# Column products for the gating input and the queries: two activation parts side by side, wide and narrow matmuls, sums on VectorE, attention calls at other slots

## The chip, the cores and the metric

The kernel runs on one core of one Trainium2 chip. The core has a matrix engine (TensorE, "PE" in the profile; its weight loads are listed apart as "PEld"), a vector engine (VectorE, "DVE"), a scalar engine (ScalarE, "ACT"), a general engine (GpSimd, "POOL") and a queue that starts transfers (SyncE, "SP"). Each works through its own instructions in order, and they wait for each other with semaphores. Matmuls write to PSUM, which has eight banks of 512 float32 per partition; everything else works in SBUF. The metric is the time of one execution on the device in microseconds (us).

## The reference

The model is a decoder trunk of two layers on 256 positions with 1024 features, in float32. A layer is an FFN, a mixing sub-layer and a second FFN, each between two RMS norms:

```
h = rms_norm(x, ffn1_pre_g);  x = x + 0.5 * rms_norm(swiglu(h, w1, w2), ffn1_post_g)
h = rms_norm(x, mix_pre_g)
q, k, v, u_s, v_s, g_a, g_b = split(h @ w_in)
y_attn = sliding_window_attention(q, k, v, sinks)        # 16 query heads, 2 key/value heads, window 128
y_sgu  = spatial_gating(gelu(u_s), gelu(v_s), ...)       # u * (tril(W) layer_norm(v) + b), chunks of 128
merged = sigmoid(g_a) * (y_attn @ w_attn_branch) + sigmoid(g_b) * (y_sgu @ w_sgu_branch)
x = x + rms_norm(merged @ w_out, mix_post_g)
h = rms_norm(x, ffn2_pre_g);  x = x + 0.5 * rms_norm(swiglu(h, ...), ffn2_post_g)
```

The change is about two of the products with `w_in`: `u_s`, the gating input, and `q`, the queries, each 1024 features wide.

## The kernel before

**Products.** A float32 product is made of three products of TensorE's rounded format (float32r). Each operand is split into a high part, its rounded copy, and a low part, the rest: x = xh + xl and w = wh + wl. The product is xh·wh + xl·wh + xh·wl. The activations of a sub-layer lie transposed in one tile `xt` of 8 blocks of 128 features, and in each block the 256 positions of the high part are followed by the 256 of the low part. Three helpers form products. `row_major` (L266, through `passes`, L254) keeps activations as the stationary operand and streams weights, and its result has positions as rows. `feature_major` (L256) and `feature_pair` (L276) keep a block of weights stationary and stream activations, and the result has features as rows. `feature_major` takes three matmuls of 256 columns for each of 8 blocks, 24 in all, and sums everything in one half of a bank (lines L261, L262 and L263). `feature_pair` streams both parts of a block at once as 512 columns against wh, and the high part as 256 columns against wl: 8 wide and 8 narrow matmuls (L284). The bank then holds two halves, which must still be added. Before the change only the middle of the FFNs (`FFN.middle`, L637) uses it: there ACT copies the second half of the bank out (L650) and DVE adds the first half to the copy (L651).

**Weights.** The stream `st` (L102 on) brings the weights in units of 128 x 1024. SP starts a transfer into one of four raw buffers, ACT makes the high part `wh` (L140), DVE the low part `wl` (L154). Nine units fit the ring, and a unit is split up to AHEAD + 1 = 8 units ahead of its product; the low part of a unit is issued when the next unit is split (`low`, L148). After its product a unit's place becomes free (`done`).

**The mixing sub-layer** (`Mix.middle`, L806) works off 48 units in numbered slots: 0 to 7 the gating input u, 8 to 15 the queries q, 16 to 23 the gate g_b, 24 to 31 the gating branch, 32 to 39 the gate g_a, 40 to 47 the attention branch. `beside` (L818) issues for a slot first what is due at its start, then the product, then what is due at its second half, and then splits the next unit. What is due is held in a table by half-slots, and `go` (L813) runs a generator until its next `yield n`, which puts the rest n half-slots later. So the order of the instructions on every engine is fixed by hand; nothing is decided at run time.

`pairs` (L831) makes two units in the two halves of one bank and then starts the evacuation at the second half of the slot after them. For u this is one Gelu on ACT into `ut` (L873). For q it is `evac_q` (L883): ACT scales the two halves of the partitions by 0.125 into the high parts (L887), and one half-slot later DVE forms the low parts (L890), so that each head gets high and low part one above the other.

In slots 9 to 12 `gating` (L700) puts 8 matmuls of 128 columns on PE (L706) ahead of the slot's product, then two DVE steps (L710, L713), an ACT copy (L715) and a DVE step (L717). The keys' two transposes (L393) come at slot 3.

`attend` (L720) is called six times per layer, for each key/value head once for the first 128 positions (eight heads in one call) and twice for the second 128 (four heads each). ATTEND (L59) holds the half-slots at which the calls start. A call issues scores on PE (L736, L737); 3 half-slots later maxima on DVE (L743); 1 later exponentials on ACT (L756); 3 later the sums on DVE and the division on POOL (L764); 4 later transposes on PE (L773), split by ACT and DVE; 5 later the products with the values on PE (L785, L786); and then four short steps on ACT and DVE. The first call of a layer needs the queries of units 0 to 3 of q.

**Buffers.** The pool `mm` (L85) has 8 banks; the pool `t2` (L79) has 6 buffers of 512 float32 per partition, which the gating, attention and FFN steps share.

Of the kernel before, what the change touches and what calls it, by code (L numbers as in the profile page):

```python
# [16 lines left out]
AF = mybir.ActivationFunctionType  # L17
ALU = mybir.AluOpType
PSUM = bass.MemoryType.PSUM

P = 128
D = 1024
KD = D // P
S = 256
# [31 lines left out]

WARM = (11, 8)

ATTEND = (27, 32, 38, 44, 50, 56)  # L59
GATING = (9, 10, 11, 12)  # L60

GATE = (31, 33)
# [3 lines left out]
def trunk(ctx: ExitStack, tc: tile.TileContext, a: dict, out: bass.AP):  # L66
    nc = tc.nc

    def pool(name, bufs, **kw):
        return ctx.enter_context(tc.tile_pool(name=name, bufs=bufs, **kw))  # L70
# [8 lines left out]
    t2 = pool("t2", 6)  # L79
# [11 lines left out]
    def new(p, shape, tag, dt=F32, **kw):  # L91
        ids[0] += 1
        return p.tile(shape, dt, tag=tag, name=f"{tag}_{ids[0]}", **kw)

    def f(ap):
        return ap.bitcast(F32)

    def flat(ap):
        return ap.rearrange("p a b -> p (a b)")
# [67 lines left out]
    st = Stream()  # L167
# [45 lines left out]
    def bank():  # L213
        return new(mm, [P, 512], "mm")
# [38 lines left out]
        for i in which:  # L253
            nc.tensor.matmul(o, every[i][0], every[i][1], start=start and i == 0, stop=stop and i == 2)  # L254

    def feature_major(o, u, ah, al):  # L256

        wh, wl = st[u]
        for k in range(KD):
            ks = slice(k * P, (k + 1) * P)  # L260
            nc.tensor.matmul(o, wh[:, ks], ah[:, k, :], start=(k == 0), stop=False)  # L261
            nc.tensor.matmul(o, wh[:, ks], al[:, k, :], start=False, stop=False)  # L262
            nc.tensor.matmul(o, wl[:, ks], ah[:, k, :], start=False, stop=(k == KD - 1))  # L263
        st.done(u)

    def row_major(o, u, m, ah, al):  # L266

        wh, wl = st[u]
        for t in range(NT):
            for i in range(2):  # L270
                k, ws = 2 * m + i, slice(i * 512, (i + 1) * 512)
                passes(o[t], ah[:, k, rows_of(t)], al[:, k, rows_of(t)], wh[:, ws], wl[:, ws], (0, 1, 2),
                       k == 0, k == KD - 1)
        st.done(u)

    def feature_pair(o, u, both):  # L276

        wh, wl = st[u]

        wide = [(o, wh, flat(both[:, k]), k) for k in range(KD)]  # L280
        narrow = [(o[:, 0:S], wl, both[:, k, 0, :], k) for k in range(KD)]
        todo = wide[:-1] + narrow + wide[-1:]
        for i, (out_, w, x, k) in enumerate(todo):
            nc.tensor.matmul(out_, w[:, k * P:(k + 1) * P], x, start=(i == 0), stop=(i == len(todo) - 1))  # L284
        st.done(u)
# [334 lines left out]
    class FFN:  # L620
# [16 lines left out]
        def middle(self, xt, xth, xtl, turn1, early):  # L637
            for _ in range(2):
                self.into.append((new(m8, [P, 8, S], "m8", F32R), new(m8, [P, 8, S], "m8", F32R)))
            for c in range(FA, FC):  # L640
                o = [bank(), bank()]
                us = self.cols[(c - FA) * 2:(c - FA) * 2 + 2]
                for half in range(2):
                    feature_pair(o[half], us[half], xt)
                if c == FA + 2:
                    turn1()
                s = new(t2, [P, 512], "t2")
                y = s.rearrange("p (a b) -> p a b", a=2)
                for half in range(2):
                    nc.scalar.copy(y[:, half, :], o[half][:, S:2 * S])  # L650
                    nc.vector.tensor_tensor(out=y[:, half, :], in0=o[half][:, 0:S], in1=y[:, half, :], op=ALU.add)  # L651
                    if half == 0:
                        nc.scalar.activation(y[:, 0, :], y[:, 0, :], AF.Silu)  # L653
                nc.vector.tensor_tensor(out=y[:, 1, :], in0=y[:, 0, :], in1=y[:, 1, :], op=ALU.mult)
                st.upto(us[1] + 1 + AHEAD)
                hh, hl = self.lhs(c)
                split(hh, hl, s[:, S:2 * S])
                if c == FA + 2:
                    early()

    class Mix:
# [144 lines left out]
        def middle(self, xt, xth, xtl, turn1, early):  # L806
# [3 lines left out]
            def at(slot, fn):  # L810
                todo.setdefault(slot, []).append(fn)

            def go(gen, half):  # L813
                wait = next(gen, None)
                if wait is not None:
                    at(divmod(half + wait, 2), lambda: go(gen, half + wait))

            def beside(product):  # L818

                for fn in todo.pop((now[0], 0), ()):  # L820
                    fn()
                u = product()
                for fn in todo.pop((now[0], 1), ()):
                    fn()
                if u in self.at:
                    st.upto(self.rows[-1] + 1, 1)
                else:
                    st.upto(u + 1 + AHEAD)
                now[0] += 1

            def pairs(units, ah, al, evac):  # L831

                for j in range(KD):
                    def product():
                        if j % 2 == 0:
                            o[:] = [bank().rearrange("p (a b) -> p a b", a=2)]
                        feature_major(o[0][:, j % 2, :], units[j], ah, al)
                        return units[j]

                    if j % 2 == 0:  # L840
                        o = [None]
                    beside(product)
                    if j % 2:
                        half = 2 * now[0] + 1
                        at(divmod(half, 2), lambda j=j, o=o[0], half=half: go(evac(j - 1, o), half))

            def quads(units, ah, al, evac):

# [20 lines left out]
            for i, slot in enumerate(GATING):  # L869
                at((slot, 0), lambda i=i, slot=slot: go(self.gating(2 * i), 2 * slot))  # L870

            def to(dst, j, o, func=AF.Copy):
                nc.scalar.activation(dst[:, j:j + 2, :], o, func)  # L873
                yield from ()

            pairs(self.u, xth, xtl, lambda j, o: to(self.ut, j, o, AF.Gelu))

# [3 lines left out]
            def evac_q(j, o):  # L883
                js = slice(j, j + 2)
                own = [(self.qs[r], slice(r * HD, (r + 1) * HD), slice((1 - r) * HD, (2 - r) * HD)) for r in range(2)]
                for q, b, _ in own:
                    nc.scalar.mul(q[b, js, :], o[b], 0.125)  # L887
                yield 1
                for q, b, other in own:
                    nc.vector.scalar_tensor_tensor(out=q[other, js, :], in0=o[b], scalar=0.125,  # L890
                                                   in1=f(q[b, js, :]), op0=ALU.mult, op1=ALU.subtract)

            calls = []
# [5 lines left out]

            for half, call in zip(ATTEND, calls):  # L900
                at(divmod(half, 2), lambda half=half, call=call: go(self.attend(*call), half))
            pairs(self.q, xth, xtl, evac_q)

            def rows_to(dst, h, t, o):
                nc.scalar.copy(dst[:, t, halves()[h]], o)
# [155 lines left out]
    sums = []  # L1061
# [13 lines left out]
    xt = both[:, :, 0, :], both[:, :, 1, :]  # L1075
    for t in range(NT):
        for h in range(2):
            ks = slice(h * 4, h * 4 + 4)
# [91 lines left out]
```

## Time and profile before

| what | value |
|---|---|
| median of 3 runs | 1179.42 us (1179.13 to 1179.55) |
| the profiled execution's own time | 1180.49 us |
| its span | 1178.8 us |
| PE busy | 1167.2 us, 99% |
| weight loads | 1007.7 us, 85% |
| DVE busy | 839.7 us, 71% |
| ACT busy | 676.8 us, 57% |
| POOL busy | 59.9 us, 5% |
| read from HBM | 218.65 MB |

Rows of groups read: line, engine, operation, output<-inputs, shapes, count | busy us, mean ns of one | idle us before, and who ended it. Rows in order of time read: start in us, duration in us, engine, line, operation, and in brackets the idle time before with who ended it; equal neighbours are merged with their count. A matmul's duration includes its passage through the array, and the next one starts before it ends, so distances between starts say what a matmul costs in a stream.

### The profile page before, as it was taken

How to read it: one execution, taken by the hardware profiler on the slowest of the kernel's cores; microseconds unless marked ns; L12 is line 12 of the kernel's file. 1: busy time of each engine (PE TensorE's matmuls, PEld its weight loads, DVE VectorE, ACT ScalarE, POOL GpSimd, SP SyncE). 2: the span in 40 equal slices, each digit the busy share in tenths (PEclk: the TensorE clock that was granted, in tenths of full speed). 3: DMA queues.
4: the chain of work that ended last, by engine and by line, in shares of the span. 5: the costliest groups of instructions: out<-in, count | busy, mean ns of one | idle time of the engine just before them, and what ended most of it. 6: DMA issues, size and time to landing. Idle time of an engine off the chain costs nothing.

```text
span 1178.8 us, 16939 instructions
## 1 busy us (share of the span) xinstructions
PE 1167.2 (99%) x6295; PEld 1007.7 (85%) x6295; DVE 839.7 (71%) x1423; ACT 676.8 (57%) x1139; POOL 59.9 (5%) x44
## 2 busy tenths in 40 slices
PE   8999999999999999999999999999999999999997
PEld 7888888999888888888888888889988888888886
DVE  6768757888787866766586666579778787676752
ACT  5657544557785455655455665455577854566551
POOL 0000000001131100000000000000021220000000
PEclk9999999999999999999999999999999999999999
DMA  7566674555457435657635667645554672565560
GB/s 250 179 242 224 229 234 162 177 181 163 159 161 250 143 140 197 200 196 259 223 106 178 232 199 248 208 152 180 178 167 142 210 222 84 179 212 198 195 199 36
DMA packets 61283, 220.81 MB, mean 187 GB/s; under 512 B 7056, under 2 KB 7056, under 8 KB 61200
## 3 DMA queue, kind: packets, MB, share of 16 engines
q1 hardware_dynamic: 60912, 219.46, 56.1%
q8 instruction: 50, 0.82, 0.3%
q14 instruction: 33, 0.27, 0.1%
q10 hardware_dynamic: 288, 0.27, 0.1%
HBM read 218.65 MB, written 1.05 MB: 186 GB/s over the span
## 4 chain that ended last, share of the span: by engine, by line
PE 98%; DVE 1%; DMA 0%; ACT 0%; issue 0%; SPq 0%; DVEq 0%
PE mm L254 51%; PE mm L284 34%; PE mm L261 3%; PE mm L262 3%; PE mm L263 3%; PE mm L219 2%; PE mm L773 1%; PE mm L737 1%; PE mm L736 1%; PE mm L706 1%; DMA raw<-in_ffn_w 0%; PE mm L786 0%; PE mm L785 0%; DVE t L1079 0%; ACT xt L1003 0%; DVE xt L1006 0%
## 5 line engine op out<-in xcount | busy, mean ns | idle before, releaser
L154 DVE TENSOR_TENSOR wl<-raw,wh 128x1024 fp32r<-128x1024 f32 x372 | 455.0, 1248 | 93.7 <-ACT wh L140 92.2
L140 ACT CAST wh<-raw 128x1024 fp32r<-128x1024 f32 x372 | 383.8, 1051 | 162.0 <-DMA raw<-in_ffn_w 78.0
L254 PE MATMUL mm<-wh,m 128*128 128x512 f32 x1088 | 341.7, 391 | 0.0
L284 PE MATMUL mm<-xt,wh 128*128 128x512 f32 x1152 | 290.5, 393 | 0.7 <-DVE xt L1006 0.7
L254 PEld LDWEIGHTS mm<-wh,m 128*128 128x128 f32 x1088 | 204.3, 188 | 41.9
L284 PEld LDWEIGHTS mm<-xt,wh 128*128 128x128 f32 x1152 | 207.2, 189 | 38.4 <-DVE xt L1006 1.2
L254 PE MATMUL mm<-wl,m 128*128 128x512 f32 x544 | 211.8, 389 | 0.0
L284 PEld LDWEIGHTS mm<-xt,wl 128*128 128x128 f32 x1152 | 157.1, 190 | 11.3
L284 PE MATMUL mm<-xt,wl 128*128 128x256 f32 x1152 | 160.6, 282 | 0.0
L254 PE MATMUL mm<-wh,xt 128*128 128x512 f32 (+1 forms) x480 | 144.1, 378 | 0.0
L651 DVE TENSOR_TENSOR t<-mm,t 128x256 f32<-128x256 f32 x144 | 60.7, 421 | 96.3 <-ACT t L650 96.2
L254 PEld LDWEIGHTS mm<-wl,m 128*128 128x128 f32 x544 | 102.2, 188 | 20.6
L254 PEld LDWEIGHTS mm<-wh,xt 128*128 128x128 f32 x480 | 88.4, 188 | 16.0
L254 PE MATMUL mm<-wl,xt 128*128 128x512 f32 (+1 forms) x240 | 87.5, 375 | 0.0
L650 ACT COPY t<-mm 128x256 f32<-128x256 f32 x144 | 53.0, 368 | 46.4 <-PE mm L284 46.2
L261 PE MATMUL mm<-xt,wh 128*128 128x256 f32 x256 | 73.3, 286 | 0.0
L653 ACT ACTIVATE t<-t 128x256 f32<-128x256 f32 x72 | 30.1, 418 | 74.3 <-DVE t L651 74.3
L263 PE MATMUL mm<-xt,wl 128*128 128x256 f32 x256 | 72.4, 283 | 0.0
L262 PE MATMUL mm<-xt,wh 128*128 128x256 f32 x256 | 72.4, 283 | 0.0
L254 PE MATMUL mm<-m,xt 128*128 128x512 f32 x216 | 54.5, 397 | 0.0
L254 PEld LDWEIGHTS mm<-wl,xt 128*128 128x128 f32 x240 | 45.2, 188 | 7.8
L764 POOL TENSOR_TENSOR t<-t,rd 128x1024 f32<-128x1024 f32 x12 | 26.0, 2170 | 506.4 <-DVE rd L763 488.7
(150 smaller groups left out, 1093.1 us busy)
## 6 DMA issues: line engine op xcount, KB each, us to landing
raw<-in_ffn_w SPq DMA_DIRECT2D x264, 512.0 KB, 4.4
raw<-in_w_in SPq DMA_DIRECT2D x84, 512.0 KB, 3.9
raw<-in_w_sgu_branch SPq DMA_DIRECT2D x16, 512.0 KB, 3.6
raw<-in_w_attn_branch SPq DMA_DIRECT2D x16, 512.0 KB, 3.9
raw<-in_w_out SPq DMA_DIRECT2D x16, 512.0 KB, 4.5
gain<-in_ffn_post_g SPq DMA_DIRECT2D x4, 512.0 KB, 6.7
gain<-in_ffn_pre_g SPq DMA_DIRECT2D x3, 512.0 KB, 5.9
x<-in_x SPq DMA_DIRECT2D x4, 256.0 KB, 4.5
```

Of the source, the lines that this page charges most:

```text
L140: nc.scalar.copy(h, self.raw[u])
L154: nc.vector.tensor_tensor(out=lo, in0=self.raw.pop(u), in1=f(h), op=ALU.subtract)
L219: nc.tensor.transpose(ps[:, k, :], src[:, (c0 + k) * P:(c0 + k + 1) * P], ident)
L254: nc.tensor.matmul(o, every[i][0], every[i][1], start=start and i == 0, stop=stop and i == 2)
L261: nc.tensor.matmul(o, wh[:, ks], ah[:, k, :], start=(k == 0), stop=False)
L262: nc.tensor.matmul(o, wh[:, ks], al[:, k, :], start=False, stop=False)
L263: nc.tensor.matmul(o, wl[:, ks], ah[:, k, :], start=False, stop=(k == KD - 1))
L284: nc.tensor.matmul(out_, w[:, k * P:(k + 1) * P], x, start=(i == 0), stop=(i == len(todo) - 1))
L650: nc.scalar.copy(y[:, half, :], o[half][:, S:2 * S])
L651: nc.vector.tensor_tensor(out=y[:, half, :], in0=o[half][:, 0:S], in1=y[:, half, :], op=ALU.add)
L653: nc.scalar.activation(y[:, 0, :], y[:, 0, :], AF.Silu)
L764: nc.gpsimd.tensor_tensor(out=p, in0=p, in1=rd[:, :nh].unsqueeze(2).to_broadcast([P, nh, nk]), op=ALU.mult)
```

## The change

Both products change from `feature_major` to `feature_pair`, and `feature_major` goes. A pair of units now takes two banks, one for each unit, whose halves hold the two partial sums. A new generator `sums` adds them: ACT copies the second halves of both banks to a `t2` buffer, one half-slot later DVE adds the first halves to it, and one half-slot later the caller goes on. The Gelu and `evac_q` then read this buffer instead of PSUM, two half-slots later than before. The six attention calls start at other half-slots: 27, 32, 38, 44, 50, 56 become 30, 35, 40, 45, 51, 57.

```diff
-ATTEND = (27, 32, 38, 44, 50, 56)
+ATTEND = (30, 35, 40, 45, 51, 57)
...
-    def feature_major(o, u, ah, al):
...
-            def pairs(units, ah, al, evac):
+            def pairs(units, evac):
                 for j in range(KD):
                     def product():
-                        if j % 2 == 0:
-                            o[:] = [bank().rearrange("p (a b) -> p a b", a=2)]
-                        feature_major(o[0][:, j % 2, :], units[j], ah, al)
+                        feature_pair(o[j % 2], units[j], xt)
                         return units[j]
                     if j % 2 == 0:
-                        o = [None]
+                        o = [bank() for _ in range(2)]
                     beside(product)
                     if j % 2:
                         half = 2 * now[0] + 1
-                        at(divmod(half, 2), lambda j=j, o=o[0], half=half: go(evac(j - 1, o), half))
+                        at(divmod(half, 2), lambda j=j, o=o, half=half: go(evac(j - 1, o), half))
+            def sums(o):
+                y = new(t2, [P, 2, S], "t2")
+                for i in range(2):
+                    nc.scalar.copy(y[:, i, :], o[i][:, S:2 * S])
+                yield 1
+                for i in range(2):
+                    nc.vector.tensor_tensor(out=y[:, i, :], in0=o[i][:, 0:S], in1=y[:, i, :], op=ALU.add)
+                yield 1
+                return y
...
-            def to(dst, j, o, func=AF.Copy):
-                nc.scalar.activation(dst[:, j:j + 2, :], o, func)
-                yield from ()
-            pairs(self.u, xth, xtl, lambda j, o: to(self.ut, j, o, AF.Gelu))
+            def evac_u(j, o):
+                y = yield from sums(o)
+                nc.scalar.activation(self.ut[:, j:j + 2, :], y, AF.Gelu)
+            pairs(self.u, evac_u)
...
+                y = yield from sums(o)
                 for q, b, _ in own:
-                    nc.scalar.mul(q[b, js, :], o[b], 0.125)
+                    nc.scalar.mul(q[b, js, :], y[b], 0.125)
                 yield 1
                 for q, b, other in own:
-                    nc.vector.scalar_tensor_tensor(out=q[other, js, :], in0=o[b], scalar=0.125,
+                    nc.vector.scalar_tensor_tensor(out=q[other, js, :], in0=y[b], scalar=0.125,
                                                    in1=f(q[b, js, :]), op0=ALU.mult, op1=ALU.subtract)
...
-            pairs(self.q, xth, xtl, evac_q)
+            pairs(self.q, evac_q)
```

More of the change, by code (lines that the diff above doesn't have):

```diff
@@ L254, in passes @@
             nc.tensor.matmul(o, every[i][0], every[i][1], start=start and i == 0, stop=stop and i == 2)
-    def feature_major(o, u, ah, al):
[L258 to L264, printed above, removed]
     def row_major(o, u, m, ah, al):
```

## The prediction

> **What bounds the kernel now.** I read the page first: the span, each engine's busy share, the chain of work that ended last. Then the waits of PE alone, then PE in order of time around the changed stage.
>
> ```profile
> span 1178.8 us, 16939 instructions
> ...
> PE 1167.2 (99%) x6295; PEld 1007.7 (85%) x6295; DVE 839.7 (71%) x1423; ACT 676.8 (57%) x1139; POOL 59.9 (5%) x44
> ...
> PE 98%; DVE 1%; DMA 0%; ACT 0%; issue 0%; SPq 0%; DVEq 0%
> ```
>
> The waits of PE (who it waited for, us in total, times, longest):
>
> ```profile
> PE mm L254 <- ACT m L140: 1.9, 1, 1.9
> PE mm L1028 <- POOL ident masks.py:199: 1.4, 1, 1.4
> PE mm L284 <- DVE xt L1006: 0.7, 1, 0.7
> ```
>
> PE is the bound, end to end: it waits three times, 4.0 us together, none of them in the mixing sub-layers that the change touches. So the time moves by what the change takes from PE's own stream, plus any wait it puts into it. The busy sums cannot price a matmul, since neighbours overlap; I take distances between starts. PE in order of time, at the old unit (start, duration, line):
>
> ```profile
> 237.62 0.28 PE L261 MATMUL mm<-xt,wh 128*128 128x256 f32 x1
> ...
> 249.14 0.28 PE L261 MATMUL mm<-xt,wh 128*128 128x256 f32 x1
> ...
> 252.83 0.36 PE L261 MATMUL mm<-xt,wh 128*128 128x256 f32 x1
> ...
> 255.79 1.06 PE L706 MATMUL mm<-wt,n 128*128 128x128 f32 x8
> ```
>
> From 237.62 to 249.14 lie four units of 24 matmuls: 11.52 / 4 = 2.880 us a unit, 0.120 us a matmul. The unit right behind a block of gating matmuls (L706) takes 255.79 - 252.83 = 2.96 us, a surcharge of 0.08. The same helper that the change now calls, in the first FFN:
>
> ```profile
> 50.09 1.12 PE L284 MATMUL mm<-xt,wl 128*128 128x256 f32 x8
> ...
> 51.27 1.03 PE L219 MATMUL mm<-ident,t 128*128 128x128 f32 x8
> 52.07 1.87 PE L284 MATMUL mm<-xt,wh 128*128 128x512 f32 x7
> 53.78 1.10 PE L284 MATMUL mm<-xt,wl 128*128 128x256 f32 x8
> ...
> 134.77 1.11 PE L284 MATMUL mm<-xt,wl 128*128 128x256 f32 x8
> ```
>
> From the narrow group at 53.78 to that at 134.77 lie 29 units: 80.99 / 29 = 2.793 us a unit, although it streams as many columns (8 x 512 + 8 x 256 = 24 x 256 = 6144). With a foreign block in between (50.09 to 53.78 is 3.69 us; the block itself 52.07 - 51.27 = 0.80) the surcharge is 3.69 - 2.79 - 0.80 = 0.10.
>
> **The change part by part.** *Matmuls.* 2 layers x 16 units lose 2.880 - 2.793 = 0.087 us each: -2.78 us, all of it on PE's stream. Foreign blocks inside this stage: the two key transposes and four gating blocks per layer, 10 in all, each with a surcharge 0.02 higher (0.10 against 0.08): +0.2 us. The blocks themselves, and the attention matmuls, keep their number and shape; the shift only places them between other units, and a block costs its surcharge wherever it stands. Sum on PE: -2.6 us, with -2.3 and -2.8 as ends, since the surcharge of 0.10 was read behind transposes and not behind gating blocks.
>
> *Sums.* Each unit adds one ACT copy of 128x256 out of PSUM and one DVE add:
>
> ```profile
> L651 DVE TENSOR_TENSOR t<-mm,t 128x256 f32<-128x256 f32 x144 | 60.7, 421 | 96.3 <-ACT t L650 96.2
> ...
> L650 ACT COPY t<-mm 128x256 f32<-128x256 f32 x144 | 53.0, 368 | 46.4 <-PE mm L284 46.2
> ```
>
> Per layer 16 x 0.421 = 6.7 us of DVE and 16 x 0.368 = 5.9 us of ACT. The Gelu and the query scaling then read SBUF where they read PSUM; I take them as equally long. The cover is what DVE and ACT have left in the stage (length; busy PE, weight load, DVE, ACT, POOL; then clock and DMA): the first row is the gating-input units, the second the query units, the third a later stretch with attention.
>
> ```profile
> 225.90:249.10 23.20, 23.20 (x196) 23.20 (x195) 20.17 (x32) 10.31 (x13) 0.00 (x0) 1.00 0.61 203
> 249.10:277.50 28.40, 28.40 (x242) 28.40 (x241) 23.77 (x44) 17.86 (x34) 0.00 (x0) 1.00 0.52 169
> 302.00:325.00 23.00, 23.00 (x119) 19.52 (x118) 18.94 (x50) 17.41 (x47) 4.82 (x3) 1.00 0.42 137
> ```
>
> ACT stays below 24 of 28 us. DVE is another matter: 20.17 + 23.77 + 6.7 = 50.7 us of work against 51.6 - 1.3 = 50.3 us of PE time. It has no air left and runs late. Weights bear that: they are split up to eight units ahead (AHEAD), some 8 x 2.8 = 22 us. New in the queues: an add on DVE waits for its ACT copy, and the query scaling on ACT waits for the add; behind them stand the weight splits (wl on DVE, wh on ACT), for which PE waits only when those 22 us are used up.
>
> *The shift.* What cannot run late is the first attention call, which needs the queries of the first four units. It moves from half-slot 27 to 30, so PE has one more unit before it; its DVE, ACT and POOL steps move along, no DMA is among them, and on POOL the order to the gate products stays. DVE ahead of this call, before the change:
>
> ```profile
> 264.58 0.68 DVE L710 TENSOR_TENSOR t<-mm,sb 128x512 f32<-128x512 f32 x1
> 265.30 0.69 DVE L713 TENSOR_TENSOR t<-t,n 128x512 f32<-128x512 f32 x1
> 265.91 0.68 DVE L717 TENSOR_TENSOR m<-t,m 128x512 fp32r<-128x512 f32 x1
> 266.51 1.22 DVE L154 TENSOR_TENSOR wl<-raw,wh 128x1024 fp32r<-128x1024 f32 x1
> 267.76 1.41 DVE L890 SCALAR_TENSOR_TENSOR m<-mm,m 64x512 fp32r<-64x512 f32 x2
> 269.20 0.69 DVE L717 TENSOR_TENSOR m<-t,m 128x512 fp32r<-128x512 f32 x1
> ```
>
> and PE, with the last gating block, the call's first matmul and its ninth, the first that reads the second pair of query units:
>
> ```profile
> 263.32 1.06 PE L706 MATMUL mm<-wt,n 128*128 128x128 f32 x8
> ...
> 269.97 0.22 PE L736 MATMUL mm<-kth,m 128*128 128x128 f32 x1
> ...
> 270.81 0.27 PE L736 MATMUL mm<-kth,m 128*128 128x128 f32 x1
> ```
>
> Today DVE ends the last query step (L890) at 267.76 + 1.41 = 269.2, 1.6 us before the ninth matmul at 270.8. By the new order DVE does, from the start of that gating block on, with distances between the starts above: the rest of a wl split and its wait (0.8 us, by going through the slots before it in the same way), L890 of the first pair 1.43, L710 0.72, L713 0.61, L717 0.60, L154 1.25, two adds 0.84, L717 0.60, L154 1.25, L890 1.41: 9.5 us. PE needs for the block 0.81, three units of 2.79 and the surcharge 9.3 us to the call and 10.1 us to its ninth matmul. So 0.6 us of slack are left of 1.6. I cost the shift at nothing; the cover is that 0.6 us, and if it is gone each further us of DVE or ACT delay is one us of PE wait per layer. The ends: 0 and +1.2 us per layer, the upper one being one more wl split (1.25) ahead of the last step and some hand-over time. Later calls stand 5 half-slots apart instead of 6 where they are densest; at six DVE is busy 18.94 of 23.00 us, so at most 18.94 x 6/5 = 22.7 of 23.0: no wait of PE from that.
>
> *Sum.* -2.6 us on the profiled execution: 1180.5 (its span 1178.8 and 1.7 around it) becomes 1177.9. That execution is 1.1 us above the median of the runs, so the median 1179.4 becomes 1176.8.
>
> **The rivals.** *A: the forecast*, the PE stream alone: 1176.8, own range 1176.5 to 1177.2.
>
> *B: a small stall.* The slack of 0.6 us is an estimate from some ten steps; if the call waits 0.2 to 1.2 us in each layer, 0.4 to 2.4 of the 2.6 us go: 1177.2 to 1179.2, middle 1178.2. For it: DVE has no idle time left in this stage. Against it: PE gets 2.8 us more ahead of the call than before.
>
> *C: only streamed columns count.* Both forms stream 6144 columns; were a matmul's cost proportional to them, PE's stream would keep its length and the time would be 1179.4. Against it: 2.793 against 2.880 us for the same columns. The Trainium skill's page "TensorE: Matmul & The Clock Gate", section "Wait — 56ns, not 53.3ns?", comes close to it: one column per cycle of 2.4 GHz plus about 2.5 ns per matmul. By that rule, as an estimate, eight matmuls fewer save 20 ns a unit and 0.6 us in all, hence 1178.8; the trace disagrees, with 0.120 us for 256 columns where the rule has 0.109.
>
> *D: slower, the query hand-over becomes the bound.* Copy, add, scaling and the second part now go ACT, DVE, ACT, DVE, and ACT casts stand between them that wait for DMA:
>
> ```profile
> 247.90 1.05 ACT L140 CAST wh<-raw 128x1024 fp32r<-128x1024 f32 x1 [2.30 <-DMA raw<-in_w_in]
> ```
>
> If one such cast (2.30 waiting, 1.05 working) gets in front of the scaling, the call comes 3.35 - 0.6 = 2.8 us late per layer, 5.5 in all: 1179.4 - 2.6 + 5.5 = 1182.3. It decides from 1.3 + 0.6 = 1.9 us of delay per layer on. Against it: by the order of the slots the casts ahead of the scaling belong to units whose data landed long before.
>
> **How the numbers follow.** Chances: A 0.64, B 0.23, C 0.03, D 0.10. What a measurement can tell from no change is about 0.2%, 2.4 us. A stands at 2.6, just beyond; with its ends of 2.3 and 2.8 I give three quarters of A to faster, 0.48. Slower by over 0.2% is D without its lower part, 0.08. The rest, 0.44, is within 0.2%: a quarter of A, B, C and the lower part of D. The range 1176.2 to 1180.2 holds A, B and C and leaves out the larger part of D.
>
> **What would show it right or wrong.** In the changed kernel: units of 2.79 us at the gating inputs and the queries, no rows of L261 to L263; units behind a gating block at 2.88 to 2.90; 32 more copies and 32 more adds at 0.37 and 0.42 us; DVE busy above 0.95 from the gating inputs to the first attention call. B and D would show as a wait of PE at the score matmuls of the first call of each layer, released by DVE's last query step; a wait of PE for wh or wl in this stage, or at a later call, would make the prediction wrong in a way that I hold unlikely. C would show as units of 2.88 us.

## The result, and the profile after

The changed kernel takes 1182.26 us (median of 15 runs, 1181.45 to 1184.2), the kernel before on the same chip 1179.25 us. The ratio is 1.0025 with an interval of 1.0017 to 1.0033: the change costs 3.0 us (2.0 to 3.9) where 2.6 us of gain were forecast. The profiled execution of the changed kernel took 1181.68 us.

Its page, first the span, then the busy shares, then the shares of the chain that ended last:

```profile
span 1179.9 us, 16487 instructions
...
PE 1164.0 (99%) x6039; PEld 992.2 (84%) x6039; DVE 851.1 (72%) x1455; ACT 684.8 (58%) x1171; POOL 63.7 (5%) x44
...
PE 93%; ACT 3%; DVE 2%; DMA 1%; POOL 1%; issue 0%; SPq 0%; DVEq 0%; POOLq 0%; ACTq 0%
```

PE is busy 3.2 us less than before, and yet the span is longer. Before, the chain lay on PE for 98% of the span; now it leaves PE for ACT, DVE and POOL. The waits of PE (who it waited for, us in total, times, longest) say where:

```profile
PE mm L254 <- ACT m L140: 2.5, 2, 2.1
PE mm L764 <- POOL t L755: 2.0, 2, 1.0
...
PE mm L727 <- DVE t L172: 1.4, 2, 0.7
```

The first row is the wait for the first weights of the program, which was there before. The other two are new, each twice, once per layer: attention's transposes (L764) wait for POOL's division (L755), and scores (L727) wait for DVE's part of a split (L172). Both lie in later attention calls and not in the first one. (One more new row, 0.3 us at L219, lies outside the mixing sub-layers; the fastest variant below has it too.)

**What came as forecast.** PE in order of time (start, duration) in the changed kernel, with the query units, then the first and the ninth matmul of the first call:

```profile
264.10 1.11 PE L275 MATMUL mm<-xt,wl 128*128 128x256 f32 x8
...
269.69 1.11 PE L275 MATMUL mm<-xt,wl 128*128 128x256 f32 x8
...
270.87 0.22 PE L727 MATMUL mm<-kth,m 128*128 128x128 f32 x1
...
271.71 0.28 PE L727 MATMUL mm<-kth,m 128*128 128x128 f32 x1
```

From 264.10 to 269.69 lie two units: 5.59 / 2 = 2.79 us each. With a gating block in between, the distance is 3.70 us (253.00 to 256.70), 0.81 of it the block, so 2.89 for the unit, as forecast. DVE's last query step ahead of the ninth matmul, in the same trace:

```profile
269.22 1.40 DVE L892 SCALAR_TENSOR_TENSOR m<-t,m 64x512 fp32r<-64x512 f32 x2
```

It ends at 270.62, 1.1 us before the ninth matmul at 271.71. The first call does not wait.

The new copies and adds (groups of the changed kernel: count, busy us, mean ns), and busy time by stretch over the gating-input and the query units (length; busy PE, weight load, DVE, ACT, POOL):

```profile
L844 DVE TENSOR_TENSOR t<-mm,t 128x256 f32<-128x256 f32 x32 | 12.0, 417 | 0.1
...
L841 ACT COPY t<-mm 128x256 f32<-128x256 f32 x32 | 10.4, 368 | 0.9 <-PE mm L275 0.9
```

```profile
225.10:247.60 22.50, 22.50 (x132) 19.80 (x131) 20.17 (x34) 9.77 (x17) 0.00 (x0) 1.00 0.60 189
247.60:275.40 27.80, 27.80 (x178) 25.08 (x177) 26.15 (x41) 19.12 (x31) 0.00 (x0) 1.00 0.61 190
```

The durations are those forecast. DVE is busy 20.17 of 22.50 us (0.90) and 26.15 of 27.80 us (0.94), and PE is busy in all of both stretches.

**Where the time went.** PE in order of time at three later places of the first layer: transposes of the fourth call, scores of the sixth call, transposes of the sixth call.

```profile
318.07 0.39 PE L777 MATMUL mm<-t,vv 128*128 128x512 f32 x1
318.61 1.09 PE L764 MATMUL mm<-ident,t 128*128 128x128 f32 x8
...
322.41 0.28 PE L728 MATMUL mm<-ktl,m 128*128 128x256 f32 x1
...
323.40 0.39 PE L727 MATMUL mm<-kth,m 128*128 128x256 f32 x1 [0.71 <-DVE t L172]
...
340.33 0.39 PE L777 MATMUL mm<-t,vv 128*128 128x512 f32 x1
341.69 1.09 PE L764 MATMUL mm<-ident,t 128*128 128x128 f32 x8 [0.98 <-POOL t L755]
```

A matmul of 512 columns is followed by the next after about 0.23 us (ahead of the fifth call's transposes, which do not wait, it is 0.24: 330.36 to 330.60), one of 256 after 0.12. So the three distances of 0.54, 0.99 and 1.36 us hold 0.30, 0.87 and 1.13 us of waiting. The second layer has the same three. That is 2.30 us per layer and 4.6 in two, and -2.6 + 4.6 = +2.0 us, the lower end of the measured interval. (The rows of waits count from the modelled end of the matmul before, so they show less, and they miss the first wait.)

Single executions differ by some 2 us. In the traces it is mostly their start that differs: PE waits between 0.77 and 3.10 us for its first weights, and in four of the twelve, that of the kernel before among them, the granted clock is 0.50 for about 3.4 us behind that wait (before, from 9.00 to 12.30 us: 0.50; the changed kernel in the same stretch: 1.00). I therefore also compare a distance that leaves the start out: from the second layer's key transposes to the last matmul of all. Before:

```profile
800.89 0.38 PE L393 MATMUL mm<-ident,t 128*128 128x128 f32 x2
...
1171.02 0.39 PE L254 MATMUL mm<-wh,m 128*128 128x512 f32 x1
```

and after:

```profile
800.70 0.38 PE L384 MATMUL mm<-ident,t 128*128 128x128 f32 x2
...
1172.14 0.39 PE L254 MATMUL mm<-wh,m 128*128 128x512 f32 x1
```

370.13 us became 371.44: +1.31 for one layer. 13 of its 16 changed units lie in this stretch.

**How the three waits come about.** The chain of waits of the changed kernel in order of time (start, us, what), from the fourth call's divisor to the sixth call's scores:

```profile
312.36 1.29 DVE t L172 x2
...
314.25 1.14 DVE wl L154
...
315.87 2.69 POOL t L755
...
320.12 0.68 ACT t L747 x3
...
321.20 0.95 ACT wh L140
322.14 0.48 ACT t L171
322.65 0.70 DVE t L172
323.40 0.39 PE mm L727
```

The fourth call now starts 5 half-slots behind the third (40 and 45), formerly 6. Its divisor stands on DVE behind the third call's split and a weight split. Its division starts at 315.87 and ends at 318.56, just when PE has run out of other work: 0.30 us. Then ACT's part of the fourth call's split (L171) stands behind exponentials of the fifth call (L747) and a weight cast (L140). DVE's part follows at 322.65, and the sixth call's scores start when the first half of it is done: 0.87 us. That these scores wait for the bank which the split reads is inferred from the order of the events.

The third wait starts on ACT, in order of time, in the changed kernel:

```profile
334.01 1.28 ACT L917 ACT_TABLE_LOAD   x1
335.30 1.06 ACT L917 ACTIVATE n<-n 128x1024 f32<-128x1024 f32 x1
336.27 1.06 ACT L171 CAST t<-mm 128x512 fp32r<-128x512 f32 x2
```

and before:

```profile
331.96 1.08 ACT L171 CAST t<-mm 128x512 fp32r<-128x512 f32 x2 [0.24 <-PE mm L773]
...
334.01 1.28 ACT L915 ACT_TABLE_LOAD   x1
```

The fifth call's transposes were at half-slot 50 + 11 = 61 and are now at 51 + 11 = 62, the start of slot 31. There stands the first sigmoid of the gate (`gate_b`, GATE = 31 and 33), with a table load. Before, ACT split the fifth call at 331.96 and then did the sigmoid; now the split comes behind it, at 336.27. The sixth call's division on POOL follows, before the change at

```profile
335.46 1.90 POOL L764 TENSOR_TENSOR t<-t,rd 128x1024 f32<-128x1024 f32 x1 [9.03 <-DVE rd L763]
```

and after it at

```profile
339.75 1.90 POOL L755 TENSOR_TENSOR t<-t,rd 128x1024 f32<-128x1024 f32 x1 [11.99 <-ACT wh L140]
```

It comes 4.3 us later, though the call itself starts only one half-slot later.

### The profile page after: what moved, and what is told of

Same layout as the page of the kernel before. It is cut to its first block, busy times and chain, and to the rows that moved or that the text cites. A ratio compares the mean times of both kernels' runs of the same rounds, so it can differ in the third digit from the quotient of the medians.

```text
span 1179.9 us, 16487 instructions
## 1 busy us (share of the span) xinstructions
PE 1164.0 (99%) x6039; PEld 992.2 (84%) x6039; DVE 851.1 (72%) x1455; ACT 684.8 (58%) x1171; POOL 63.7 (5%) x44
## 4 chain that ended last, share of the span: by engine, by line
PE 93%; ACT 3%; DVE 2%; DMA 1%; POOL 1%; issue 0%; SPq 0%; DVEq 0%; POOLq 0%; ACTq 0%
PE mm L254 46%; PE mm L275 42%; PE mm L219 1%; PE mm L764 1%; POOL t L755 1%; ACT wh L140 1%; PE mm L727 1%; PE mm L728 1%; PE mm L697 1%; DMA raw<-in_ffn_w 1%; DVE wl L154 1%; DMA raw<-in_w_in 0%; ACT t L747 0%; ACT t L171 0%; DVE t L172 0%
## 5 line engine op out<-in xcount | busy, mean ns | idle before, releaser
L154 DVE TENSOR_TENSOR wl<-raw,wh 128x1024 fp32r<-128x1024 f32 x372 | 456.8, 1250 | 85.9 <-ACT wh L140 84.1
L140 ACT CAST wh<-raw 128x1024 fp32r<-128x1024 f32 x372 | 383.7, 1053 | 145.5 <-DMA raw<-in_ffn_w 68.4
L275 PE MATMUL mm<-xt,wh 128*128 128x512 f32 x1408 | 357.9, 393 | 0.7 <-DVE xt L1008 0.7
L275 PEld LDWEIGHTS mm<-xt,wh 128*128 128x128 f32 x1408 | 253.2, 189 | 46.0 <-DVE xt L1008 1.2
L275 PEld LDWEIGHTS mm<-xt,wl 128*128 128x128 f32 x1408 | 192.1, 190 | 13.9
L275 PE MATMUL mm<-xt,wl 128*128 128x256 f32 x1408 | 196.3, 282 | 0.0
L755 POOL TENSOR_TENSOR t<-t,rd 128x1024 f32<-128x1024 f32 x12 | 27.6, 2299 | 514.8 <-DVE rd L754 459.7
L254 PEld LDWEIGHTS mm<-m,xt 128*128 128x128 f32 x216 | 39.4, 188 | 10.5 <-ACT xt L530 2.1
L747 ACT ACTIVATE t<-t,nm 128x128 f32<-128x128 f32 (+1 forms) x64 | 28.3, 444 | 24.9 <-DVE nm L738 24.9
L172 DVE TENSOR_TENSOR m<-t,m 128x256 fp32r<-128x256 f32 x72 | 30.2, 420 | 15.5 <-ACT m L171 15.5
```

What stands on the lines that cost most here:

```text
L140: nc.scalar.copy(h, self.raw[u])
L154: nc.vector.tensor_tensor(out=lo, in0=self.raw.pop(u), in1=f(h), op=ALU.subtract)
L172: nc.vector.tensor_tensor(out=lo, in0=src, in1=f(h), op=ALU.subtract)
L747: nc.scalar.activation(p[:, i, :], p[:, i, :], AF.Exp, bias=nm[:, i:i + 1], accum_out=sm[:, i:i + 1])
L755: nc.gpsimd.tensor_tensor(out=p, in0=p, in1=rd[:, :nh].unsqueeze(2).to_broadcast([P, nh, nk]), op=ALU.mult)
```

## The experiments

The theory after the result: the products and the sums behave as forecast, and the new positions of the calls put steps of ACT, DVE and POOL behind others in their queues (order). The rival: the copies and adds fill DVE and ACT so that the later calls run late (work). The first three runs part the two, the others take the waits apart.

**The shift alone**, on the kernel before:

```diff
-ATTEND = (27, 32, 38, 44, 50, 56)
+ATTEND = (30, 35, 40, 45, 51, 57)
```

> The kernel before with nothing changed but the half-slots of the six attention calls (30, 35, 40, 45, 51, 57). Theory H: the shift is what costs. In the changed kernel PE waits three times per layer, behind the transposes of the fourth and sixth call and ahead of the scores of the sixth, 0.30 + 1.13 + 0.87 = 2.3 us a layer, 4.6 in all. By H this kernel shows the same three waits and is 4 to 5 us slower than before. Rival R: the sums' ACT and DVE work makes the calls late; by R the shift alone is free, and this kernel is within 1 us of before.

Measured: 1184.62 us against 1179.74, ratio 1.0042 (1.0029 to 1.0055), +4.9 us. The waits of PE:

```profile
PE mm L773 <- POOL t L764: 2.0, 2, 1.0
...
PE mm L736 <- DVE t L172: 1.4, 2, 0.7
```

These are the waits of the changed kernel, to a tenth of a microsecond, without one copy or add of the new kind. The distance that leaves out the start:

```profile
802.34 0.38 PE L393 MATMUL mm<-ident,t 128*128 128x128 f32 x2
...
1175.08 0.39 PE L254 MATMUL mm<-wh,m 128*128 128x512 f32 x1
```

372.74 us, +2.61 for one layer. Order makes the loss, and work is not needed for it.

**The products alone.** The changed kernel with the old half-slots and without the sums: Gelu and query scaling read only the first half of each bank, so the products with the low part of the activations are formed but not added.

```diff
-ATTEND = (30, 35, 40, 45, 51, 57)
+ATTEND = (27, 32, 38, 44, 50, 56)
...
-                y = yield from sums(o)
-                nc.scalar.activation(self.ut[:, j:j + 2, :], y, AF.Gelu)
+                for i in range(2):
+                    nc.scalar.activation(self.ut[:, j + i, :], o[i][:, 0:S], AF.Gelu)
...
```

> The wide and narrow matmuls alone, with the attention calls at their old half-slots; the second halves of the banks are left out (no sums), and Gelu and query scaling read the first halves, one unit at a time. By both theories PE's stream gets 2.6 us shorter and nothing waits: 2.3 to 2.8 us faster than before. If a matmul's cost went by columns alone, no change.

Measured: 1176.94 us against 1179.74, ratio 0.9977 (0.9967 to 0.9987), -2.8 us. The distance:

```profile
798.88 0.38 PE L384 MATMUL mm<-ident,t 128*128 128x128 f32 x2
...
1167.68 0.39 PE L254 MATMUL mm<-wh,m 128*128 128x512 f32 x1
```

368.80 us, -1.33 for one layer. With the +2.61 of the shift alone the sum is +1.28, and the changed kernel shows +1.31: the two parts add up and nothing is left for the sums. (The 2.61 are 0.3 more than the three waits; where these 0.3 lie was not traced.)

**The sums without their two steps of delay**, at the old half-slots: all that the change computes, but the copies, adds and scaling follow each other at once.

```diff
-ATTEND = (30, 35, 40, 45, 51, 57)
+ATTEND = (27, 32, 38, 44, 50, 56)
...
             def sums(o):
...
-                yield 1
...
-                yield 1
```

> The changed kernel, but the sums are issued without the two half-slots between their steps, which puts the query steps where they stood before, and the attention calls stand at the old half-slots 27, 32, 38, 44, 50, 56. Theory H: the three waits are gone; what is left is a wait at the first call of 0 to 1.2 us per layer, so 0.2 to 2.6 us faster than before. Rival R (the added ACT and DVE work costs): about 2 us slower than before, as the changed kernel.

Measured: 1178.28 us against 1179.74, ratio 0.9984 (0.9976 to 0.9993), -1.5 us. The first call does not wait, although it starts three half-slots earlier than in the changed kernel. PE is left with one short wait in each layer, at a later call's scores, of 0.26 us in the first and 0.53 us in the second by distances between starts. They make up 0.8 of the 1.3 us by which this kernel stays behind the products alone.

**The gate's sigmoids later**, in the changed kernel:

```diff
-GATE = (31, 33)
+GATE = (33, 35)
```

> The changed kernel with the two sigmoids of the gate g_b two slots later (slots 33 and 35 for 31 and 33). Theory H says that the wait at the sixth call's transposes comes from the fifth call's split, which now stands behind the first sigmoid and its table load on ACT; with the sigmoid out of its way 1.1 us per layer go, so this kernel is 2 us faster than the changed one, about 1 us slower than before. By R (all calls late for lack of DVE time) it stays within 0.5 us of the changed one, 3 us slower than before.

Measured: 1179.98 us against 1179.74, ratio 1.0001 (0.9991 to 1.001). The waits for POOL's division are gone from the list, the two at the sixth call's scores stay (1.4 us in all). The distance that leaves out the start is 370.21 us (802.42 to 1172.64), 1.23 shorter than in the changed kernel, about the 1.13 us of the third wait. So the third wait comes from the sigmoid in front of the split.

**The changed kernel again**, beside the following runs.

> The changed kernel itself, once more beside the others on the same chip. The parts measured alone give -2.8 + 4.9 = +2.1 us; the first measurement gave +3.0 (interval +2.0 to +3.9). If the parts add up, +2 to +2.6 us; if the sums cost about 1 us beyond the shift, +3 us again.

Measured: 1182.12 us against 1179.62, ratio 1.0022 (1.0013 to 1.0031), +2.5 us, with the same three waits. The distance that leaves out the start is 371.41 us (801.91 to 1173.32), where the first execution had 371.44.

**The old pattern moved as a whole.** In the changed kernel all six calls start 4 half-slots later than they did before, and the sigmoids 2 slots later, which is as much:

```diff
-ATTEND = (30, 35, 40, 45, 51, 57)
+ATTEND = (31, 36, 42, 48, 54, 60)
-GATE = (31, 33)
+GATE = (33, 35)
```

> The changed kernel with the old spacing of the attention calls, all shifted by the same even number of half-slots (31, 36, 42, 48, 54, 60 = the old places plus 4), and the gate's sigmoids shifted by the same two slots (33, 35). Theory H: no wait of PE behind or ahead of any attention call is left, and the sums cost nothing: -2.6 to -2.8 us against before, as the products alone measured. Rival R2: the sums' ACT and DVE work itself keeps 1 us or more (the version with the old slots and compressed sums reached only -1.5): then -1 to -2 us.

Measured: 1176.97 us against 1179.62, ratio 0.9979 (0.997 to 0.9987), -2.65 us. All four rows of PE's waits:

```profile
PE mm L254 <- ACT m L140: 1.5, 2, 1.3
PE mm L1030 <- POOL ident masks.py:199: 1.4, 1, 1.4
PE mm L275 <- DVE xt L1008: 0.7, 1, 0.7
PE mm L219 <- DVE t L456: 0.3, 1, 0.3
```

No call waits in either layer. The distance:

```profile
798.02 0.38 PE L384 MATMUL mm<-ident,t 128*128 128x128 f32 x2
...
1166.77 0.39 PE L254 MATMUL mm<-wh,m 128*128 128x512 f32 x1
```

368.75 us, as with the products alone (368.80): with all sums in place the whole forecast gain is there. This version beats both kernels. The changed kernel's 371.44 us are 2.69 longer: 2.30 us are its three waits, and where the other 0.39 lie was not traced.

**Only the later calls spread out**; the first three stay as the change put them:

```diff
-ATTEND = (30, 35, 40, 45, 51, 57)
+ATTEND = (30, 35, 40, 46, 52, 58)
-GATE = (31, 33)
+GATE = (33, 35)
```

> The changed kernel with the fourth to sixth call one half-slot later (46, 52, 58) and the sigmoids at 33 and 35. Theory H: six half-slots between the third and the fourth call give the division on POOL the time that five do not, so the wait behind the fourth call's transposes (0.30 us a layer) goes; the fourth call's transposes and the sixth call's scores then stand in one gap between units, as before the change, and the wait for their banks (0.87) goes too: -2.6 us against before. If the bank wait hangs on something else, it stays, and the result is -0.8 us.

Measured: 1176.97 us against 1179.62, ratio 0.9977 (0.9969 to 0.9986), and no call waits. So the 5 half-slots between the first, second and third call cost nothing; the loss lies in the places of the fourth to sixth call and of the sigmoids.

**Only the fourth call one half-slot later**, one execution:

```diff
-ATTEND = (30, 35, 40, 45, 51, 57)
+ATTEND = (30, 35, 40, 46, 51, 57)
```

> The changed kernel with the fourth call alone one half-slot later (46 for 45). Theory H: of the three waits per layer that of 0.30 us behind the fourth call's transposes and that of 0.87 us ahead of the sixth call's scores go, and the one of 1.13 us behind the sixth call's transposes stays, since it hangs on the sigmoid at slot 31: 2.3 us of PE waits in the two layers instead of 4.6.

Measured: 1186.0 us, the longest of all. The first row of PE's waits:

```profile
PE mm L764 <- POOL t L755: 4.9, 2, 2.5
```

and PE at the sixth call's transposes in the first layer:

```profile
340.37 0.39 PE L777 MATMUL mm<-t,vv 128*128 128x512 f32 x1
343.22 1.09 PE L764 MATMUL mm<-ident,t 128*128 128x128 f32 x8 [2.46 <-POOL t L755]
```

The waits of 0.30 and 0.87 us are gone, as expected. But the wait at the sixth call's transposes, which was to stay at 1.13 us, more than doubled, to 2.85 - 0.23 = 2.62 us by distances: the expectation missed. A short wait of 0.25 us within the fourth call's transposes is new, so a layer now waits 2.87 us instead of 2.30. The waits are not a sum of independent terms. Measured from the first call's division (284.12 us in the changed kernel, 285.19 here), PE is ready for the sixth call's transposes 1.03 us sooner, and their division starts 0.45 us later (341.27 against 339.75), which together are the 1.49 us by which the wait grew. Why the division starts later was not traced.

Not all of the 1186.0 us is waiting. In the second layer the granted clock behind this wait is 0.50 from 926.10 to 929.40 us, and matmuls of 512 columns lie 0.43 us apart instead of 0.23; by these distances some 1.6 us go there. Behind the equally long wait of the first layer it is 1.00 (343.30 to 347.00 us). This is one execution, so its time says less than its waits.

**Both single edits**, the fourth call and the sigmoids:

```diff
-ATTEND = (30, 35, 40, 45, 51, 57)
+ATTEND = (30, 35, 40, 46, 51, 57)
-GATE = (31, 33)
+GATE = (33, 35)
```

> The changed kernel with two numbers altered: the fourth call at 46 for 45, and the sigmoids at slots 33 and 35 for 31 and 33. Theory H': each number carries one of two separate causes (46: too few half-slots for the division on POOL, and banks held by the transposes when the scores come; 33: the fifth call's split behind the sigmoid on ACT). With the fourth call alone moved, PE came earlier to the sixth call's transposes and waited 2.46 us there, so only both together help: no wait of PE at any call, -2.6 us against before. If the sixth call's chain is late for another reason (DVE work as such), a wait of 1 us or more per layer stays there.

Measured: 1178.88 us against 1179.01, ratio 0.9999 (0.9989 to 1.0008). This missed as well: -2.6 us had been expected. The distance that leaves out the start is 369.56 us (800.52 to 1170.08), -0.57 for one layer where the even pattern has -1.38. Part of the rest is in short waits of 0.26 us within the fourth call's transposes and 0.30 us before the sixth call's. The fifth call is now only 5 half-slots behind the fourth, which is probably the reason: the kernel with all later calls spread out differs from this one only in the fifth and the sixth call, one half-slot later, and shows neither wait (368.84 us, 798.59 to 1167.44). The fifth call was not moved by itself. By the distances this kernel should be about 1.1 us faster than before, by the runs it is 0.1 us faster (1.3 faster to 0.9 slower); the two agree within the interval, but not better.

**The sigmoid half a slot later**, one execution:

```diff
-                at((slot, 0), lambda h=h, slot=slot: go(gate_b(h), 2 * slot))
+                at((slot, 1), lambda h=h, slot=slot: go(gate_b(h), 2 * slot + 1))
```

> The changed kernel with the sigmoids one half-slot later, at the second half of slots 31 and 33 in place of their start, so that they are issued right behind the fifth call's split in place of ahead of it; everything else as in the changed kernel. Theory H': it is the order of these two on ACT that decides, so the wait behind the sixth call's transposes (1.13 us a layer) goes or nearly so, and the other two (0.30 and 0.87) stay: 2.3 us of PE waits at the calls in place of 4.6. If it is the sigmoid's work as such, most of the wait stays.

Measured: 1179.85 us against 1179.01. The sixth call's division on POOL:

```profile
337.26 1.90 POOL L755 TENSOR_TENSOR t<-t,rd 128x1024 f32<-128x1024 f32 x1 [9.62 <-ACT n L917]
```

It comes 2.5 us earlier than the 339.75 of the changed kernel, and PE no longer waits there; the other two waits stay. The distance that leaves out the start is 370.24 us (800.13 to 1170.37), 1.20 shorter than in the changed kernel. Only the two sigmoids and the gate products that follow them were moved here, by half a slot, the first sigmoid to behind the fifth call's split. So it is this order that makes the third wait.

## Why the prediction was wrong

*Matmuls: right.* The units take 2.79 us, and the products alone gain 2.8 us (1.5 to 3.9) where 2.6 were forecast. In the second layer's stretch the 13 units in it should give 13 x 0.087 = 1.1 us and the trace has 1.33; where the other 0.2 come from was not traced. Rival C fell with this: the same columns in fewer matmuls do cost less.

*Sums: right.* They cost nothing that PE sees: the old pattern moved as a whole has all of them and is as fast as the products alone. The statement that DVE has no air left was too strong. It was forecast to be busy above 0.95 and is at 0.90 and 0.94. The sum of 50.7 us took over the old query stretch with the eight maxima of the first call (L743, 2.3 us); of these only two still fall into the new one.

*The shift, first call: right.* There is no wait; the slack is 1.1 us instead of 0.6. This was the place of rivals B and D, and both fell: neither a small stall nor a late query hand-over shows in any run.

*The shift, later calls: the step that failed.* The prediction put it so: "Later calls stand 5 half-slots apart instead of 6 where they are densest; at six DVE is busy 18.94 of 23.00 us, so at most 18.94 x 6/5 = 22.7 of 23.0: no wait of PE from that." It priced the new positions by a busy share, and by that of DVE alone. A busy share says whether an engine can do its work at all. It does not say when a given step gets its turn in a queue that is worked off in order. What the runs show in its place is 2.30 us of waits per layer. 1.17 of them come from the fourth call, whose division and split stand behind steps of the third and fifth call. 1.13 come from the fifth call's split, which moved past the gate's sigmoid and its table load on ACT. By the distances a further 0.3 to 0.4 us per layer are lost in none of the three waits; their cause stays open. Neither needs an engine without idle time: on ACT the step that came late had been held up by 1.28 + 1.06 us of one other operation. The sentence that the order to the gate products stays was true of POOL, and only POOL was looked at; on ACT the order changed. The range missed the time because its upper end came from rivals B and D at the first call. A wait at a later call was named among the signs, as unlikely, but it got no case, no price and no chance. Rival D's figure of 1182.3 us is what was measured, but by luck: its mechanism is not what happened.

*The largest effect was thus an edit costed at nothing.* By itself it costs 4.9 us, and moved in a way that keeps the pattern it costs nothing.

## What to carry to other kernels

Where the order of the queues is written by hand, price a moved step by who stands ahead of it on each engine at its new place, for every step that it issues and for its neighbours' too; a busy share is no answer, and one engine's order says nothing of another's. If a step must move, move the whole pattern that it is part of by the same amount: here that gave 1176.97 us where the partial shift gave 1182.26. Waits along one chain do not add up, so the ones seen in the trace can be removed and the sum of waits still grows: from 2.30 to 2.87 us per layer in the one execution with the fourth call alone.

## What the runs showed of the hardware

POOL's division of 1024 elements per partition takes 1.90 us or about 2.7 us in 142 of the 144 cases in the twelve traces. It is the long form exactly when DVE was already running a weight split (L154, two inputs in SBUF) as the division began. The other two cases, in the kernel without the two steps of delay, take 2.29 us (at 281.08 us in the first layer): there DVE had just begun a query step (L891, 0.69 us, two inputs in SBUF as well). In the changed kernel, POOL at the fourth and the fifth call:

```profile
315.87 2.69 POOL L755 TENSOR_TENSOR t<-t,rd 128x1024 f32<-128x1024 f32 x1 [10.10 <-DVE rd L754]
...
325.86 1.90 POOL L755 TENSOR_TENSOR t<-t,rd 128x1024 f32<-128x1024 f32 x1 [7.30 <-ACT t L787]
```

and the weight splits on DVE beside them:

```profile
315.61 1.19 DVE L154 TENSOR_TENSOR wl<-raw,wh 128x1024 fp32r<-128x1024 f32 x1
...
326.71 2.13 DVE L154 TENSOR_TENSOR wl<-raw,wh 128x1024 fp32r<-128x1024 f32 x1
```

In the first pair DVE began first, and POOL took 0.79 us longer. In the second POOL began first, and the split took 2.13 us where it otherwise takes about 1.2. The Trainium skill's page "SBUF — State Buffer", section "Who interferes with whom", gives a rule for this: DVE and GpSimd share one pair of ports under an exclusive lock, a DVE instruction with two SBUF inputs contends with a GpSimd instruction that reads SBUF, and whichever was issued first blocks the other. The traces agree. At 1.90 us the fourth call's division would have ended at 317.8, before PE wanted it at 318.3. So the lock may be all of the first wait, on top of the order that makes the division late; this is worked out from the rows and was not tried. With the later calls spread out the same division still takes 2.69 us, and PE does not wait for it.
